# Compressed attention on column and row groups of TensorE, and a last piece without splitting and attention steps

## The chip, the cores and the metric

The kernel runs on one core of a Trainium2 chip. The metric is device time in microseconds (us), the median of several executions of the same program. A core has a matrix engine (TensorE; PE in the profile, with the loading of weights as PEld), a vector engine (VectorE, DVE), a scalar engine (ScalarE, ACT), a general one (GpSimd, POOL) and a queue engine (SyncE, SP) that issues the DMAs here. TensorE writes to PSUM only, eight banks of 128 x 512 float32; VectorE and ScalarE read the banks out.

## The reference

Two layers of a decoder trunk on 256 tokens of width 2048, all in float32. Each layer normalises its input, projects it to 6992 columns, runs four groups of four heads (128 wide), multiplies each group by a gate, projects back and adds the normalised result to the input:

```python
h = rms_norm(x, pre_g)
p = split_columns(h @ w_in + b_in)
o_sb  = stick_breaking_attention(...)      # group A
o_nsa = native_sparse_attention(...)       # group B
o_fox = forgetting_attention(...)          # group C
o_mla = latent_attention(...)              # group D
mix = concatenate([o_g * silu(gate_g) for each group])
return x + rms_norm(mix @ w_out, post_g)
```

Group B is the one that the change touches. It adds three branches, each with a gate per token and head. The compressed branch first makes 15 short keys and values out of blocks of 32 tokens (two small matrix products per block), and then attends to them:

```python
zc = einsum("bqhd,bnd->bhqn", qb, kc) * scale            # n: 15 compressed keys
pc = masked_softmax(zc, cmp_end[None, :] <= qpos[:, None])
o_cmp = einsum("bhqn,bnd->bqhd", pc, vc)
...
return gb[..., 0:1] * o_cmp + gb[..., 1:2] * o_slc + gb[..., 2:3] * o_win
```

The selected branch (o_slc) and the window branch (o_win) are plain causal attention at this length.

## The kernel before, in words

**Weight matmuls.** The large products use weights that are split into two parts, `whi` and `wlo`, so that TensorE can take them in its faster float32 form. A piece is 256 rows by 512 columns of weights. SP loads it into one of four `raw` buffers, ScalarE rounds each half (128 rows) to `whi`, VectorE subtracts to `wlo`, and TensorE uses the piece: 2.8 us of matmuls. Eight split pieces fit on chip. The class `Stream` keeps the counts: `his` and `los` are the halves split so far, `used` the pieces taken by TensorE, `loaded` the pieces asked for. When both halves of a piece are split, its raw buffer is free and SP loads the next piece (`loads`); small loads that wait in `side`, the compression's first weights among them, go out one with each piece.

A chunk of 512 columns of the input projection is eight pieces. There are two kinds. A transposed chunk (`t_group`, blocks "T", lines L634 and L635) has four blocks of 128 columns; each block has a PSUM bank of its own, and in each piece it takes two pairs of matmuls, 512 and 256 columns streamed. In the last piece (`ks == 7`) the blocks are finished one after the other, and `evac` reads each bank out: ScalarE copies one half (`tpart`), VectorE adds the other (`tgrp`), POOL multiplies by the norm factor. Then a task is spawned that adds the bias on ScalarE, and this reads POOL's product. The other kind (`k_group`, blocks "K", line L646) has tokens on the partitions and two banks. There are four such banks (`mm`), used in turn. The chunk of the compressed tokens (`nsa_kv`) has two T blocks and one K2 block, and its evacuation has the bias in it.

The order of chunks in a layer: cq and ckv of the latent group (K, 8 pieces), nsa q (K), 4 pieces of small up projections, mlag (T), nsa window keys (K), compressed and selected tokens (T, T, K2), nsag (T), sb q (T), sb k (T), sb v (K), sbg (T), fox q (T), fox k (T), fox v (K), foxg (T); then the output projection, four columns of eight pieces (L646), whose pieces 7 and 8 want the products of the fox heads.

**Order of work.** The program is one list of instructions per engine, written out by a planner at build time. After each pair or triple of matmuls `pump` moves the planned TensorE time on, then calls `step`, which runs the next due step of one task (attention heads, biases, gates, softmax of the compressed branch), and `Stream.tick`, which may split one half of a piece. Due times come from a simple cost per instruction (`Timed`, `count`, `pe`); every instruction of VectorE, ScalarE and POOL is recorded at line L119 of the helper, so these are told apart by their tiles. Engines take their lists in order, so a step that waits holds up what stands behind it on its engine.

**The compressed branch** (`nsa_cmp`, `nsa_heads`). When the compressed keys `kcT` and the rotated queries `nqT` are there, eight matmuls (L1214, one per 128 tokens and head) load 128 columns of queries as weights and stream the 32 key columns, 32 columns of one bank each. VectorE adds the mask, takes the maximum, subtracts, ScalarE exponentiates, VectorE sums, inverts, multiplies by the gate and scales, POOL multiplies by the mask. In the next step two transposes (L1237) turn the result, and one copy brings it to `pcT`: partitions 32h to 32h+31 hold head h. Float32 matmuls are two instructions each, transposes one. Two lanes (`lanes`, one per pair of heads) then each take an `op` bank and an `sp` bank. For each head the lane does one matmul on 32 rows (L1253, `tile_position=(32 * h, 0)`), then attends in the selected and the window branch (`attend`: L748 scores, softmax, L780 transposes, L792 and L793 values), all into its `op` bank. Other small products that the text names: L1102, the compression's first product, 32 weight columns on four column groups; L748 on `rT`, the rotary part of the latent scores, 64 rows on two row groups.

Of the kernel before, what the change touches and what calls it, by code (L numbers as in the profile page):

```python
# [10 lines left out]
F32 = mybir.dt.float32  # L11
# [8 lines left out]
S = 256  # L20
P = 128
# [81 lines left out]
class Timed:  # L103


    def __init__(self, kr, eng, key, base, per):
        self.kr, self.eng, self.key, self.base, self.per = kr, eng, key, base, per
# [54 lines left out]
class Stream:  # L162
# [55 lines left out]
    def lo(self):  # L218
# [8 lines left out]
        if kk == 1:  # L227
            del self.raw[p]
            self.loads()

    def tick(self, n=1):
        top = 2 * min(self.freed + self.BUFS - self.spare, len(self.specs))
        for _ in range(n):
            late = self.los - 2 * self.used < 4
            if self.los < self.his - (self.his < top and not late) and (late or self.kr.behind("v") < LAG):
                self.lo()
            if self.his < top and (late or self.kr.behind("s") < LAG) and self.here():
                self.hi()
# [21 lines left out]
class Kernel:  # L260
# [4 lines left out]
    def __init__(self, nc, tc, a, pools):  # L265
        self.nc, self.tc, self.a = Engines(self, nc), tc, a
        self.__dict__.update(pools)
        self.pt = self.dep = 0.0
        self.clk = {"v": 0.0, "s": 0.0, "g": 0.0}
        self.tasks = []  # L270
        self.negr = None
        self.free = {"sp": 2, "op": 2}
        self.freed = []
        self.done = Done(self)
        self.cols_of, self.ncols_of, self.fb, self.ci = {}, {}, {}, {}
        self.hcat, self.turn = {}, {}


    def pump(self, ns):
        self.pt += ns  # L280
        self.step()
        self.ws.tick()

    def now(self, at=0.0):

# [273 lines left out]
    def chunk(self, blocks, evac):  # L559

        acc = self.accs(len(blocks))
        for ks in range(NK // 2):
            last = ks == NK // 2 - 1
            hi, lo = self.ws.get()
            for i, (b, o) in enumerate(zip(blocks, acc)):
                if b[0] == "T":
                    self.mm_t(o, hi, lo, b[1], ks)
                elif b[0] == "K":  # L570
                    self.mm_k(o[:, :b[3]], self.h_at(ks, b[1]), hi, lo, b[2], b[3], ks == 0, last)
                else:
                    for t in range(2):
                        self.mm_k(o[:, t * S:(t + 1) * S], self.h_at(ks, t), hi, lo, b[1], S, ks == 0 and t == 0, last)
                if last:
                    self.now()
                    evac(i, o)
            self.ws.free()

    def first_chunk(self, l, cols):  # L580
# [224 lines left out]
        self.split(self.mxh[g][:, hp * 2:hp * 2 + 2, :], self.mxl[g][:, hp * 2:hp * 2 + 2, :], m3)  # L805
        self.done.add((l, "mix", g, hp))

    def lanes(self, l, g, heads, need=(), banks=1):


        for hp in range(2):
            def lane(task, hp=hp):
                for key in need:
                    yield from self.until(task, key)
                yield from self.take(task, "op")
                yield from self.take(task, "sp", banks)
                o = self.bank("op")
                o = [o[:, hh * S:(hh + 1) * S] for hh in range(2)], o
                yield from heads(hp, o[0])
                self.give("sp", banks)  # L820
                yield from self.until(task, (l, "gate", g, hp))
                self.mix(l, g, hp, o[1])
                self.give("op")
            self.spawn(lane)
# [376 lines left out]
    def nsa_cmp(self, l):  # L1201

        nc = self.nc

        def probs(task):
            for key in ("cmp", "nsa_q"):
                yield from self.until(task, (l, key))
            yield from self.take(task, "sp")
            qT = self.nqT
            cp = self.bank("sp")  # L1210
            for t in range(2):
                for h in range(4):
                    a = (t * 4 + h) * 32
                    nc.tensor.matmul(cp[:, a:a + 32], qT[:, h * S + t * P:h * S + (t + 1) * P],  # L1214
                                     self.kcT[:, :32], start=True, stop=True)
            self.pe(1700)
            pc = self.t256("pc").rearrange("p (g n) -> p g n", n=32)
            for t in range(2):
                nc.vector.tensor_add(pc[:, t * 4:(t + 1) * 4, :],
                                     cp[:, t * 128:(t + 1) * 128].rearrange("p (h n) -> p h n", h=4),  # L1220
                                     self.c3("cadd", 2)[:, t, None, :].to_broadcast([P, 4, 32]))
            mx = self.sm.tile([P, 8], F32, name="cmx")
            nc.vector.tensor_reduce(mx, pc, axis=AX.X, op=OP.max)
            nc.vector.tensor_sub(pc, pc, mx[:, :, None].to_broadcast([P, 8, 32]))
            nc.scalar.activation(pc, pc, AF.Exp, scale=SCALE)
            su = self.sm.tile([P, 8], F32, name="csu")
            nc.vector.tensor_reduce(su, pc, axis=AX.X, op=OP.add)
            nc.vector.reciprocal(su, su)
            su2 = su.rearrange("p (t h) -> p t h", t=2)
            nc.vector.tensor_mul(su2, su2, self.br[:, :, :, 0])  # L1230
            nc.vector.tensor_mul(pc, pc, su[:, :, None].to_broadcast([P, 8, 32]))
            for t in range(2):
                nc.gpsimd.tensor_mul(pc[:, t * 4:(t + 1) * 4, :], pc[:, t * 4:(t + 1) * 4, :],
                                     self.c3("cmul", 2)[:, t, None, :].to_broadcast([P, 4, 32]))
            yield 0
            for t in range(2):
                nc.tensor.transpose(cp[:, t * P:(t + 1) * P],  # L1237
                                    pc[:, t * 4:(t + 1) * 4, :].rearrange("p h n -> p (h n)"), self.ident)
            self.pe(220)
            self.pcT = self.zp.tile([P, S], F32, name="pcT", bufs=1)  # L1240
            nc.vector.tensor_copy(self.pcT, cp[:, :S])
            self.give("sp")
            yield 0
            self.done.add((l, "nsa_c"))

        self.spawn(probs)

    def nsa_heads(self, nb):
        def heads(hp, o):
            for hh in range(2):  # L1250
                h = 2 * hp + hh
                r = slice(32 * h, 32 * h + 32)
                self.nc.tensor.matmul(o[hh], self.vc[r, :], self.pcT[r, :], start=(hh == 0), stop=False,  # L1253
                                      skip_group_check=True, tile_position=(32 * h, 0))
                self.pe(430)
                q = self.nqT[:, h * S:(h + 1) * S]
                yield from self.attend([([(q, self.nkT[:, 0, :])], o[hh], self.sel[:, 0, P:], self.sel[:, 1, P:],
                                         False, False, self.br[:, :, h, 1])], SCALE)
# [205 lines left out]
    def layer(self, l, xsrc, dst):  # L1464
# [7 lines left out]
        nb = self.k_group(l, CHUNKS[3])  # L1472
# [6 lines left out]
        self.nsa_kv(l)  # L1479
        self.nsa_keys(l, nb)  # L1480
        self.nsa_cmp(l)
        self.lanes(l, "nsa", self.nsa_heads(nb), [(l, "nsa_k"), (l, "nsa_c")])
        self.t_group(l, ci["nsag"], gate="nsa")
        q, qd = self.t_group(l, 124, scale=SCALE)
        k, kd = self.t_group(l, ci["sbqk"] + 4)
# [86 lines left out]
```

## Time and profile before

| | |
|---|---|
| median of 3 runs | 946.74 us (946.71 to 946.87) |
| the profiled execution's own time | 946.79 us |
| its span, first to last instruction | 944.7 us |
| mean granted TensorE clock over the span | 0.998 |
| PE busy | 922.3 us, 98% of the span, 5170 instructions |
| DVE, ACT, POOL busy | 63%, 55%, 14% |
| DMA | 178.7 MB, mean 189 GB/s |

Busy is the time in which at least one instruction of an engine is under way. Matmuls overlap in the pipeline, so the mean duration of one is longer than the distance from its start to the next start; the latter is what a stream of matmuls costs. In the lists of instructions a row gives start, duration, engine, line, operation, tiles written and read, shape and count; a bracket behind it gives the idle time of the engine just before and what ended it.

### The profile page before, as it was taken

How to read it: one execution, taken by the hardware profiler on the slowest of the kernel's cores; microseconds unless marked ns; L12 is line 12 of the kernel's file. 1: busy time of each engine (PE TensorE's matmuls, PEld its weight loads, DVE VectorE, ACT ScalarE, POOL GpSimd, SP SyncE). 2: the span in 40 equal slices, each digit the busy share in tenths (PEclk: the TensorE clock that was granted, in tenths of full speed). 3: DMA queues.
4: the chain of work that ended last, by engine and by line, in shares of the span. 5: the costliest groups of instructions: out<-in, count | busy, mean ns of one | idle time of the engine just before them, and what ended most of it. 6: DMA issues, size and time to landing. Idle time of an engine off the chain costs nothing.

```text
span 944.7 us, 14519 instructions
## 1 busy us (share of the span) xinstructions
PE 922.3 (98%) x5170; PEld 783.0 (83%) x5170; DVE 598.7 (63%) x1293; ACT 519.2 (55%) x1170; POOL 133.3 (14%) x204
## 2 busy tenths in 40 slices
PE   7999999999999999999999999999999999999996
PEld 6888988777888888888878998887778888888885
DVE  6776757646666655754586867676366675567552
ACT  7745644645467563754476564555255775457540
POOL 0231011012011212100002310212010221020000
PEclk9999999999999999999999999999999999999999
DMA  8857746784454755489268577287744545746852
GB/s 271 264 177 193 216 139 182 238 256 125 118 160 125 242 190 156 149 275 309 93 200 271 159 188 228 78 249 227 224 115 131 156 142 183 232 146 200 281 187 89
DMA packets 118080, 178.70 MB, mean 189 GB/s; under 512 B 15996, under 2 KB 40568, under 8 KB 118008
## 3 DMA queue, kind: packets, MB, share of 16 engines
q1 hardware_dynamic: 118008, 177.78, 60.5%
q8 instruction: 40, 0.66, 0.3%
q14 instruction: 32, 0.26, 0.1%
HBM read 173.55 MB, written 4.20 MB: 188 GB/s over the span
## 4 chain that ended last, share of the span: by engine, by line
PE 86%; DMA 5%; DVE 4%; ACT 2%; POOL 1%; issue 1%; SPq 1%; POOLq 0%; DVEq 0%; ACTq 0%
PE mm L646 41%; PE mm L634 22%; PE mm L635 11%; PE sp L748 2%; DMA w<-nsa_cmp_w_v 2%; PE mm L942 2%; DVE wlo L119 2%; PE op L792 1%; DMA raw<-w_in 1%; PE sp L780 1%; DMA fcum<-frow 1%; DMA w<-nsa_cmp_w_k 1%; PE op L793 1%; PE sp L482 1%; ACT whi L119 1%
## 5 line engine op out<-in xcount | busy, mean ns | idle before, releaser
L119 DVE TENSOR_TENSOR wlo<-raw,whi 128x512 fp32r<-128x512 f32 (+2 forms) x592 | 389.2, 702 | 66.7 <-ACT whi L119 64.4
L634 PE MATMUL mm<-hcat,whi 128*128 128x512 f32 x1088 | 397.3, 406 | 1.7 <-DVE tgrp L119 1.3
L119 ACT ACTIVATE whi<-raw 128x512 fp32r<-128x512 f32 (+2 forms) x592 | 330.1, 613 | 118.5 <-DMA raw<-w_in 66.7
L635 PE MATMUL mm<-hcat,wlo 128*128 128x256 f32 x1088 | 304.3, 280 | 0.0
L634 PEld LDWEIGHTS mm<-hcat,whi 128*128 128x128 f32 x1088 | 204.6, 188 | 51.1 <-issue 3.7
L646 PE MATMUL mm<-whi,hcat 128*128 128x512 f32 (+2 forms) x768 | 230.5, 371 | 0.8 <-DVE tgrp L119 0.8
L635 PEld LDWEIGHTS mm<-hcat,wlo 128*128 128x128 f32 x1088 | 205.4, 189 | 0.4
L646 PEld LDWEIGHTS mm<-whi,hcat 128*128 128x128 f32 x768 | 139.2, 189 | 22.4 <-DVE tgrp L119 2.0
L646 PE MATMUL mm<-wlo,hcat 128*128 128x512 f32 (+2 forms) x384 | 139.1, 362 | 1.4 <-DVE wlo L119 1.3
L646 PE MATMUL mm<-whi,mxh 128*128 128x512 f32 x256 | 99.8, 390 | 0.0
L646 PE MATMUL mm<-whi,mxl 128*128 128x512 f32 x256 | 99.6, 389 | 0.0
L646 PE MATMUL mm<-wlo,mxh 128*128 128x512 f32 x256 | 99.6, 389 | 0.0
L646 PEld LDWEIGHTS mm<-wlo,hcat 128*128 128x128 f32 x384 | 72.7, 189 | 11.8 <-DVE wlo L119 3.0
L119 POOL TENSOR_TENSOR tgrp<-tgrp,rr 128x256 f32<-128x256 f32 x64 | 59.6, 955 | 162.2 <-DVE tgrp L119 162.0
L119 ACT ACTIVATE z<-z,nm 128x128 f32<-128x128 f32 x64 | 28.5, 447 | 55.2 <-DVE nm L119 54.1
L646 PEld LDWEIGHTS mm<-whi,mxl 128*128 128x128 f32 x256 | 48.0, 188 | 10.1
L646 PEld LDWEIGHTS mm<-whi,mxh 128*128 128x128 f32 x256 | 48.1, 188 | 10.0
L646 PEld LDWEIGHTS mm<-wlo,mxh 128*128 128x128 f32 x256 | 48.1, 188 | 9.8
L119 DVE TENSOR_TENSOR tgrp<-mm,tpart 128x256 f32<-128x256 f32 x64 | 26.0, 419 | 40.3 <-ACT tpart L119 40.0
L119 ACT ACTIVATE tpart<-mm 128x256 f32<-128x256 f32 x68 | 24.6, 381 | 40.7 <-PE mm L635 38.7
L119 DVE TENSOR_TENSOR y<-mm,bct 128x512 f32<-128x512 f32 x16 | 11.1, 692 | 48.1 <-ACT junk L119 48.1
L119 ACT ACTIVATE junk<-mm 128x512 f32<-128x512 f32 x16 | 9.6, 598 | 52.4 <-PE mm L646 52.4
(212 smaller groups left out, 766.7 us busy)
## 6 DMA issues: line engine op xcount, KB each, us to landing
raw<-w_in SPq DMA_DIRECT2D x207, 512.0 KB
raw<-w_out SPq DMA_DIRECT2D x64, 512.0 KB
x<-x SPq DMA_DIRECT2D x24, 256.0 KB
raw<-w_in SPq DMA_DIRECT2D x16, 268.0 KB
w<-nsa_cmp_w_k SPq DMA_DIRECT2D x8, 512.0 KB
w<-nsa_cmp_w_v SPq DMA_DIRECT2D x8, 512.0 KB
raw<-mla_w_uq SPq DMA_DIRECT2D x6, 384.0 KB
bct<-b_in SPq DMA_DIRECT2D x8, 256.0 KB
```

The lines of the kernel that those rows point to most:

```text
L119: return f(out, *args, **kw)
L482: nc.tensor.transpose(ps[:, k * P:(k + 1) * P], x[:, k * P:(k + 1) * P], self.ident)
L634: nc.tensor.matmul(o, wh, h, start=(ks + kk == 0), stop=False, skip_group_check=True)
L635: nc.tensor.matmul(o[:, :S], wl, h[:, :S], start=False, stop=last, skip_group_check=True)
L646: nc.tensor.matmul(o, x, w, start=(first and kk == 0 and i == 0), stop=(last and kk == 1 and i == 2), skip_group_check=True)
L748: nc.tensor.matmul(sp[:, a:a + s1], q[:, q0:q0 + P], k[:, :s1], start=(i == 0 and a == 0), stop=(i == n - 1), skip_group_check=True)
L780: nc.tensor.transpose(sp[:, i * P:(i + 1) * P], z[:, i * P:(i + 1) * P], self.ident)
L792: nc.tensor.matmul(o, v0, pt[:, :256], start=start, stop=False, skip_group_check=True)
L793: nc.tensor.matmul(o[:, 128:256], v1, pt[:, 256:384], start=False, stop=stop, skip_group_check=True)
L942: nc.tensor.matmul(o, a, b, start=(i == 0 and o is first[0]), stop=(i == len(mms) - 1), skip_group_check=True)
```

## The change

In `nsa_cmp` the scores are turned around: four matmuls, one per head, load the 32 key columns as weights and stream the head's 256 query columns. Each writes 32 partitions of the same bank columns, on its own column group of the array. VectorE copies the result out, two more transposes bring tokens to the partitions, and the softmax goes on as before with the heads in the order 0, 2, 1, 3; the gate is multiplied in two instructions. After the softmax `pcT` is 64 partitions by 512 columns, written by two copies: partitions 32hp to 32hp+31 and column half hh hold head 2hp+hh. A new task `nsa_open` takes both `op` banks and opens each with one matmul on 32 rows and 512 columns (row groups 0 and 32); the lanes get their bank from it and do no value matmul of their own. In `chunk`, `hold` is true while a T block of the last piece is computed; then `pump` runs neither a step nor a tick, unless `short` says that fewer than three pieces beyond the one in use are split.

```diff
--- before.py
+++ after.py
@@ -228,6 +228,10 @@
             del self.raw[p]
             self.loads()
 
+    def short(self):
+
+        return self.los - 2 * self.used < 6
+
     def tick(self, n=1):
         top = 2 * min(self.freed + self.BUFS - self.spare, len(self.specs))
         for _ in range(n):
@@ -269,6 +273,7 @@
         self.clk = {"v": 0.0, "s": 0.0, "g": 0.0}
         self.tasks = []
         self.negr = None
+        self.hold = False
         self.free = {"sp": 2, "op": 2}
         self.freed = []
         self.done = Done(self)
@@ -278,8 +283,9 @@
 
     def pump(self, ns):
         self.pt += ns
-        self.step()
-        self.ws.tick()
+        if not self.hold or self.ws.short():
+            self.step()
+            self.ws.tick()
 
     def now(self, at=0.0):
 
@@ -565,6 +571,8 @@
             last = ks == NK // 2 - 1
             hi, lo = self.ws.get()
             for i, (b, o) in enumerate(zip(blocks, acc)):
+
+                self.hold = last and b[0] == "T"
                 if b[0] == "T":
                     self.mm_t(o, hi, lo, b[1], ks)
                 elif b[0] == "K":
@@ -575,6 +583,7 @@
                 if last:
                     self.now()
                     evac(i, o)
+            self.hold = False
             self.ws.free()
 
     def first_chunk(self, l, cols):
@@ -805,16 +814,17 @@
         self.split(self.mxh[g][:, hp * 2:hp * 2 + 2, :], self.mxl[g][:, hp * 2:hp * 2 + 2, :], m3)
         self.done.add((l, "mix", g, hp))
 
-    def lanes(self, l, g, heads, need=(), banks=1):
+    def lanes(self, l, g, heads, need=(), banks=1, opened=None):
 
 
         for hp in range(2):
             def lane(task, hp=hp):
                 for key in need:
                     yield from self.until(task, key)
-                yield from self.take(task, "op")
+                if opened is None:
+                    yield from self.take(task, "op")
                 yield from self.take(task, "sp", banks)
-                o = self.bank("op")
+                o = self.bank("op") if opened is None else opened[hp]
                 o = [o[:, hh * S:(hh + 1) * S] for hh in range(2)], o
                 yield from heads(hp, o[0])
                 self.give("sp", banks)
@@ -1208,16 +1218,22 @@
             yield from self.take(task, "sp")
             qT = self.nqT
             cp = self.bank("sp")
+
+            for h in range(4):
+                g = 64 * (h % 2) + 32 * (h // 2)
+                nc.tensor.matmul(cp[g:g + 32, :S], self.kcT[:, :32], qT[:, h * S:(h + 1) * S], start=True, stop=True,
+                                 tile_position=(0, g), skip_group_check=True)
+            self.pe(650)
+            cs = self.t256("cs")
+            nc.vector.tensor_copy(cs, cp[:, :S])
+            yield 0
             for t in range(2):
-                for h in range(4):
-                    a = (t * 4 + h) * 32
-                    nc.tensor.matmul(cp[:, a:a + 32], qT[:, h * S + t * P:h * S + (t + 1) * P],
-                                     self.kcT[:, :32], start=True, stop=True)
-            self.pe(1700)
+                nc.tensor.transpose(cp[:, S + t * P:S + (t + 1) * P], cs[:, t * P:(t + 1) * P], self.ident)
+            self.pe(220)
             pc = self.t256("pc").rearrange("p (g n) -> p g n", n=32)
             for t in range(2):
                 nc.vector.tensor_add(pc[:, t * 4:(t + 1) * 4, :],
-                                     cp[:, t * 128:(t + 1) * 128].rearrange("p (h n) -> p h n", h=4),
+                                     cp[:, S + t * 128:S + (t + 1) * 128].rearrange("p (h n) -> p h n", h=4),
                                      self.c3("cadd", 2)[:, t, None, :].to_broadcast([P, 4, 32]))
             mx = self.sm.tile([P, 8], F32, name="cmx")
             nc.vector.tensor_reduce(mx, pc, axis=AX.X, op=OP.max)
@@ -1227,7 +1243,9 @@
             nc.vector.tensor_reduce(su, pc, axis=AX.X, op=OP.add)
             nc.vector.reciprocal(su, su)
             su2 = su.rearrange("p (t h) -> p t h", t=2)
-            nc.vector.tensor_mul(su2, su2, self.br[:, :, :, 0])
+            for hh in range(2):
+                nc.vector.tensor_mul(su2[:, :, 2 * hh:2 * hh + 2], su2[:, :, 2 * hh:2 * hh + 2],
+                                     self.br[:, :, hh:hh + 3:2, 0])
             nc.vector.tensor_mul(pc, pc, su[:, :, None].to_broadcast([P, 8, 32]))
             for t in range(2):
                 nc.gpsimd.tensor_mul(pc[:, t * 4:(t + 1) * 4, :], pc[:, t * 4:(t + 1) * 4, :],
@@ -1237,22 +1255,37 @@
                 nc.tensor.transpose(cp[:, t * P:(t + 1) * P],
                                     pc[:, t * 4:(t + 1) * 4, :].rearrange("p h n -> p (h n)"), self.ident)
             self.pe(220)
-            self.pcT = self.zp.tile([P, S], F32, name="pcT", bufs=1)
-            nc.vector.tensor_copy(self.pcT, cp[:, :S])
+            self.pcT = self.t512("pcT")[:64, :]
+            for hh in range(2):
+                nc.vector.tensor_copy(self.pcT[:, hh * S:(hh + 1) * S], cp[64 * hh:64 * hh + 64, :S])
             self.give("sp")
             yield 0
             self.done.add((l, "nsa_c"))
 
         self.spawn(probs)
+
+    def nsa_open(self, l, nb, need):
+
+
+        def opening(task):
+            for key in need:
+                yield from self.until(task, key)
+            yield from self.take(task, "op", 2)
+            os = [self.bank("op") for _ in range(2)]
+            for hp in range(2):
+                r = slice(32 * hp, 32 * hp + 32)
+                self.nc.tensor.matmul(os[hp], self.vc[r, :], self.pcT[r, :], start=True, stop=False,
+                                      skip_group_check=True, tile_position=(32 * hp, 0))
+            self.pe(1200)
+            self.lanes(l, "nsa", self.nsa_heads(nb), opened=os)
+            yield 0
+
+        self.spawn(opening)
 
     def nsa_heads(self, nb):
         def heads(hp, o):
             for hh in range(2):
                 h = 2 * hp + hh
-                r = slice(32 * h, 32 * h + 32)
-                self.nc.tensor.matmul(o[hh], self.vc[r, :], self.pcT[r, :], start=(hh == 0), stop=False,
-                                      skip_group_check=True, tile_position=(32 * h, 0))
-                self.pe(430)
                 q = self.nqT[:, h * S:(h + 1) * S]
                 yield from self.attend([([(q, self.nkT[:, 0, :])], o[hh], self.sel[:, 0, P:], self.sel[:, 1, P:],
                                          False, False, self.br[:, :, h, 1])], SCALE)
@@ -1479,7 +1512,7 @@
         self.nsa_kv(l)
         self.nsa_keys(l, nb)
         self.nsa_cmp(l)
-        self.lanes(l, "nsa", self.nsa_heads(nb), [(l, "nsa_k"), (l, "nsa_c")])
+        self.nsa_open(l, nb, [(l, "nsa_k"), (l, "nsa_c")])
         self.t_group(l, ci["nsag"], gate="nsa")
         q, qd = self.t_group(l, 124, scale=SCALE)
         k, kd = self.t_group(l, ci["sbqk"] + 4)
```

## Rows read from the trace of the kernel before

**Rows 1.** The page, busy time, share of the span and instructions of each engine.
```profile
PE 922.3 (98%) x5170; PEld 783.0 (83%) x5170; DVE 598.7 (63%) x1293; ACT 519.2 (55%) x1170; POOL 133.3 (14%) x204
```

**Rows 2.** Waits of TensorE by releaser: total us, times, longest us.
```profile
PE op L1102 <- DMA w<-nsa_cmp_w_v: 2.3, 4, 0.8
...
PE mm L646 <- DVE wlo L119: 1.3, 1, 1.3
PE mm L634 <- DVE tgrp L119: 1.3, 2, 0.6
PE sp L1237 <- POOL pc L119: 0.9, 2, 0.5
PE mm L646 <- DVE tgrp L119: 0.8, 1, 0.8
```

**Rows 3.** Timeline of TensorE, the score matmuls in layer 0.
```profile
211.34 0.28 PE L635 MATMUL mm<-hcat,wlo 128*128 128x256 f32 x1
211.46 1.87 PE L1214 MATMUL sp<-cmp,nqT 128*128 128x32 f32 x16
...
213.48 0.27 PE L635 MATMUL mm<-hcat,wlo 128*128 128x256 f32 x1
```

**Rows 4.** Timeline of TensorE, value matmul with scores behind it; values alone; scores alone.
```profile
220.88 0.27 PE L635 MATMUL mm<-hcat,wlo 128*128 128x256 f32 x1
221.09 0.69 PE L1253 MATMUL op<-pcT,cmp 32*128 32x256 f32 x2
...
222.28 0.58 PE L646 MATMUL mm<-whi,hcat 128*128 128x512 f32 x1
...
230.51 0.59 PE L792 MATMUL op<-pt,sn 128*128 128x256 f32 x2
230.94 0.27 PE L793 MATMUL op<-pt,sn 128*128 128x128 f32 x1
...
231.62 0.40 PE L646 MATMUL mm<-whi,hcat 128*128 128x512 f32 x1
231.85 0.82 PE L748 MATMUL sp<-sn,nqT 128*128 128x128 f32 x4
232.32 0.58 PE L646 MATMUL mm<-whi,hcat 128*128 128x512 f32 x1
```

**Rows 5.** Timeline of TensorE, two row groups (L748 on rT) and four column groups (L1102).
```profile
119.37 0.93 PE L748 MATMUL sp<-rT 64*128 64x128 f32 x8
120.22 0.38 PE L646 MATMUL mm<-whi,hcat 128*128 128x256 f32 x1
...
206.26 0.28 PE L635 MATMUL mm<-hcat,wlo 128*128 128x256 f32 x1
206.38 0.40 PE L634 MATMUL mm<-hcat,whi 128*128 128x512 f32 x1
206.61 0.28 PE L635 MATMUL mm<-hcat,wlo 128*128 128x256 f32 x1
206.82 0.64 PE L1102 MATMUL op<-w,blk 128*32 128x128 f32 x16
...
207.73 0.28 PE L635 MATMUL mm<-hcat,wlo 128*128 128x256 f32 x1
```

**Rows 6.** Timeline of TensorE, the pair of transposes in layer 1.
```profile
686.14 0.38 PE L1237 MATMUL sp<-ident,pc 128*128 128x128 f32 x2
```

**Rows 7.** Timeline of TensorE, sb q to sb k in layer 1.
```profile
653.63 0.27 PE L635 MATMUL mm<-hcat,wlo 128*128 128x256 f32 x1
654.53 0.50 PE L634 MATMUL mm<-hcat,whi 128*128 128x512 f32 x1 [0.63 <-DVE tgrp L119]
```

**Rows 8.** Timeline of ScalarE, the same stretch.
```profile
653.24 0.51 ACT L119 ACTIVATE tgrp<-tgrp,cols 128x256 f32<-128x256 f32 x1 [1.69 <-POOL tgrp L119]
```

**Rows 9.** Instructions on tile wlo by stretch: length, busy (x count), PEclk, DMA share, GB/s.
```profile
0.00:159.40 159.40, 93.91 (x304) 57.81 (x304) 66.19 (x106) 1.00 0.69 210
...
0.00:380.30 380.30, 225.90 (x752) 142.28 (x753) 157.34 (x239) 1.00 0.62 190
```

## The prediction

> **What bounds the kernel now.** I read the page's busy times first: TensorE is busy 98% of the span, VectorE 63%, ScalarE 55% [rows 1], and the granted clock is at its full level of 2.4 GHz (1.00 in the stretches of [rows 9]). So the first question for any edit is how much TensorE time it takes out; work on another engine counts only where TensorE waits for it. The list of TensorE's waits, read second, says where that is: a few places of one to three microseconds in total, each with its releaser [rows 2]. Third I read TensorE's timeline around the lines that the change touches. To price an insertion I take the time from the start of the last weight matmul before it to the start of a weight matmul behind it, less the undisturbed steps: 0.12 us from a 256-column weight matmul to the next start and 0.23 us from a 512-column one (206.26, 206.38, 206.61 in [rows 5]).
>
> **Part 1, the compressed branch on column and row groups.** Old price per layer. The eight score matmuls (L1214; 16 instructions, each loads 128 columns of weights to stream 32): 211.34 to 213.48 is 2.14 us, less 0.12 + 0.23, so 1.78 us [rows 3]. The four value matmuls (L1253) each stand ahead of four L748 instructions: 220.88 to 222.28 less 0.12 is 1.28 us. The same four L748 alone cost 231.62 to 232.32 less 0.23, 0.47 us, so one value matmul costs 0.81 us. Of that, two passes of 256 columns are 0.43 us (L792 shows two, 230.51 to 230.94), and 0.38 us is getting into the 32-row form and out of it [rows 4]. Together 1.78 + 4 x 0.81 = 5.02 us per layer.
>
> New price per layer. (a) Four score matmuls, 32 weight columns each, 256 streamed columns, on four column groups. The trace has this form with 128 streamed columns: L1102, 16 instructions, 206.61 to 207.73 less 0.35, 0.77 us [rows 5]. A pass of 128 columns is half of 0.215, so 16 of them in line would be 1.7 us: the four groups run side by side, four rounds of 0.11 or 0.43 us, with 0.34 us of entry and exit. The new form is two rounds of 0.215, again 0.43 + 0.34 = 0.77 us. With no overlap at all it is 8 x 0.215 + 0.34 = 2.06 us. (b) Two more transposes: the pair at L1237 is done in 0.38 us from the first start to the last end, one of them still in the pipe when the next matmul starts [rows 6]. I take two passes of 0.11, 0.22 us; bounds 0.1 and 0.4. (c) Two value matmuls of 512 columns on two row groups, each into its own bank. The nearest row is L748 on rT: 64 rows, two row groups, two banks, eight instructions, of which four stream 128 and four 256 columns. In line they would be 1.30 us; the next matmul starts after 0.85 us [rows 5], which is half of 1.30 and 0.2 more. So row groups overlap too. Two rounds of 512 columns are 0.86 us; with the 0.38 us of entry and exit 1.24 us; in line 2.10 us. New sum 0.77 + 0.22 + 1.24 = 2.23 us, or 4.38 us with no overlap. The gain is 2.79 us per layer, 5.6 us in all; the floor is 1.3 us.
>
> What this part adds elsewhere lies beside TensorE: two copies and one small multiply on VectorE, at its mean of 598.7 / 1293 = 0.46 us some 1.4 us per layer, on an engine that is idle 37% of the time [rows 1]. It costs something only where a transpose reaches TensorE before the copy or product that it reads. The trace has that once, at L1237, where POOL's product came late: 0.9 us of waiting in the two transposes of layer 0 [rows 2], nothing in layer 1 (the pair of [rows 6] has no wait before it). The branch has one step more now, and its steps are put off in a last piece; that can spare this wait or add one in the other layer. I take 0, bounds -0.9 and +1.3. The opening takes both `op` banks at once where each lane took one; what is queued behind it are the two lanes alone, which need both open anyway.
>
> The Trainium skill, page TensorE: Matmul & The Clock Gate, section Part 3: Packing small matmuls — row/col tiling, says that a weight load overlaps running matmuls only where its row group differs. All column groups use the same rows, so by that rule the eight passes of (a) stand in line with their weight loads (an estimate from the page: 32 columns over 1.2, 27 ns each), 8 x 0.242 + 0.34 = 2.3 us. The 16 passes of L1102 in 0.77 us [rows 5] speak against it; it is kept as a rival.
>
> **Part 2, nothing but evacuation in the last piece.** At the end of a transposed chunk ScalarE and VectorE empty four banks, one every 0.7 us (two pairs of 0.35), and the next transposed chunk wants the first of them at once, 2.1 us after its matmuls, and then one every 0.7 us. Now a task step slips in between. At 653.24 ScalarE runs the bias of block 0, for which it waited 1.69 us until POOL's product was there, and the evacuation of block 1 stands behind it in ScalarE's queue [rows 8]. TensorE then finds its bank unread: 653.63 to 654.53 is 0.90 us where 0.12 is due, so 0.78 us, of which 0.63 are shown as waiting [rows 7] and 0.15 are the restart. The list has two such waits of L634 for tgrp, 1.3 us, and one of L646, 0.8 us [rows 2]; with three restarts 1.3 + 0.8 + 0.5 = 2.6 us. With no step in that stretch ScalarE has nothing else to wait for, and 2.1 us is room for two short instructions. I take all 2.6 us; bounds 0 and 3.2 (the wait for cmpT, whose bias is part of the evacuation itself and stays, may shrink too).
>
> What covers the splitting that is put off is the lead of split pieces. At 380.30, when the last piece of the last input chunk begins, 239 halves are split and 116 pieces begun, so 3.5 pieces are ready; at 159.40 it is 106 halves and 52 pieces, one piece [rows 9]. `short` lets the splitting go on where fewer than three are ready, so the hold does not act at the second place, and at the first the lead falls by at most one piece of 2.8 us to 2.5. That hides it; with a lead under one, each half would show as a wait of 1.3 us, like the one for `wlo` in [rows 2]. The steps of the forgetting heads that are put off in that piece end in the output projection, whose seventh and eighth piece want them, 16 and 19 us in (12 matmuls of 0.23 us a piece): room for 2.8 us.
>
> What is late next are the loads of the compression's first weights. TensorE waits for the values' part four times, 2.3 us [rows 2], and part of that stands behind two of the removed waits. If these loads do not come sooner, the 0.8 us before them is only waited for later, in both layers 1.6 us. If the raw buffers behind which they are queued come free with the faster evacuation, nothing is lost. I take half, +0.8 us; bounds +3 (a held half gives its raw buffer back a piece later, and the loads behind it on SP's queue start later) and -1.
>
> **Sum.** -5.6 - 2.6 + 0 + 0.8 = -7.4 us. The profiled execution took 946.79 us (span 944.7), the median of the runs is 946.74, so both give the same base: 939.4 us.
>
> **Rivals.**
> 1. The groups do not overlap in the new shapes (longer streams; 32 rows instead of 64). Part 1 then gives 1.3 us and the time is 946.8 - 1.3 - 1.8 = 943.7 us. Against it stand L1102 and rT. By the page's rule, in (a) alone, 1.5 us a layer are lost: 939.4 + 3.0 = 942.4 us. Chance of the two together 0.08.
> 2. The waits for banks come back as others, the loads (+2.2 over what I took) and POOL (+1.3): 942.9 us. Or the hold does not do what it says, because `short` is true at most chunk ends, and part 1 alone is left: 941.2 us. For it, the four waits for w1; against it, the lead at 380.30. Chance 0.17.
> 3. Slower: splits that were put off come too late, and TensorE waits for `wlo` behind chunk ends, 1.3 us each. Eighteen chunks have transposed blocks. It takes six such waits to eat the 7.4 us and eight to be slower by more than a measurement can tell; at ten the time is 952 us. For it, the lead of one piece at 159.40; against it, 3.5 pieces, 9.8 us of matmuls, at 380.30. Chance 0.05.
>
> **How the numbers follow.** Forecast 0.70, by itself 936 to 942 (the bounds of the hold and the loads). For 8 in 10 I reach over rivals 1 and 2: 935.5 to 943.5. What a measurement here can tell from no change is 0.2%, 1.9 us, so faster is all below 944.9: the forecast and nearly all of rivals 1 and 2, 0.93; same 0.03; slower 0.04.
>
> **What would show it.** The scores' group costs 0.8 us instead of 1.78, and the values are one group of 1.2 us per layer instead of four of 0.8. The waits of L634 and L646 for tgrp are gone from the list, and in a last piece no bias stands between two evacuations. The prediction is wrong if TensorE waits for `wlo` behind chunk ends, if the waits of L1102 for its loads pass 6 us, or if the new groups take the 2 us that they would in line.

## The result and the profile after

The changed kernel takes 935.35 us (934.27 to 937.24, 4 runs), against 946.74 us before: a ratio of 0.988 (95% interval 0.9866 to 0.989), 11.4 us less. Forecast were 939.4 us and a range of 935.5 to 943.5. The direction was right and the two mechanisms were those named; the gain was 4 us larger than the forecast, and the time lies just below the range.

The page of the profile after, busy times (its span is 935.5 us):

```profile
PE 916.1 (98%) x5150; PEld 780.7 (83%) x5150; DVE 592.6 (63%) x1299; ACT 521.9 (56%) x1170; POOL 118.7 (13%) x204
```

TensorE is as much the bound as before [rows 1]; there is only less of it. The lines have moved: L634 is now L643, L646 is L655, L1102 is L1112, L1237 is L1255; the scores (L1214 before) are L1224, the new transposes L1231, the values (L1253 before) L1277.

TensorE's timeline in layer 0, the new groups: start, duration, engine, line, operation and tiles.

```profile
211.44 0.27 PE L644 MATMUL mm<-hcat,wlo 128*128 128x256 f32 x1
211.65 0.64 PE L1224 MATMUL sp<-nqT,cmp 128*32 128x256 f32 x8
212.21 0.50 PE L643 MATMUL mm<-hcat,whi 128*128 128x512 f32 x1
212.55 0.28 PE L644 MATMUL mm<-hcat,wlo 128*128 128x256 f32 x1
...
212.90 0.28 PE L644 MATMUL mm<-hcat,wlo 128*128 128x256 f32 x1
213.02 0.38 PE L1231 MATMUL sp<-ident,cs 128*128 128x128 f32 x2
213.16 0.48 PE L643 MATMUL mm<-hcat,whi 128*128 128x512 f32 x1
213.47 0.28 PE L644 MATMUL mm<-hcat,wlo 128*128 128x256 f32 x1
...
221.12 0.39 PE L655 MATMUL mm<-whi,hcat 128*128 128x512 f32 x1
221.44 1.13 PE L1277 MATMUL op<-pcT,cmp 32*128 32x512 f32 x4
222.49 0.50 PE L655 MATMUL mm<-whi,hcat 128*128 128x512 f32 x1
222.83 0.40 PE L655 MATMUL mm<-wlo,hcat 128*128 128x512 f32 x1
```

Priced as in [rows 3 to 5], the scores cost 211.44 to 212.55 less 0.35, 0.76 us. The pair of transposes delays the next matmul from 213.02 to 213.16 and that one's successor by 0.08 more (213.47, where 213.39 would be undisturbed), 0.22 us. The values cost 221.12 to 222.49 less 0.23 and, with 0.11 behind them (222.83 instead of 222.72), 1.25 us. Forecast were 0.77, 0.22 and 1.24. The Trainium skill (TensorE: Matmul & The Clock Gate, Part 3: Packing small matmuls — row/col tiling) says that weight loads overlap running matmuls only where the row groups differ. By the prediction's estimate from that rule the scores would have cost 2.3 us. The trace does not bear the rule out for column groups, and the measurement decides: the eight weight loads of the scores start between 211.64 and 211.69, while the first four matmuls, started at 211.65 to 211.67, run until 212.05 (single records of the trace, which the view merges into one row).

TensorE's waits after, by releaser: total us, times, longest.

```profile
PE op L1112 <- DMA w<-nsa_cmp_w_v: 3.0, 4, 1.5
...
PE mm L655 <- DVE wlo L119: 1.5, 2, 1.3
...
PE mm L655 <- DVE tgrp L119: 0.3, 1, 0.3
PE op L1112 <- DMA w<-nsa_cmp_w_k: 0.2, 1, 0.2
```

Beside [rows 2], the waits of 2.1 us for tgrp are down to 0.3, the 0.9 us for POOL at the transposes of pc is gone, the 0.3 us each for cmpT and z are gone, and the loads of w take 3.2 us, where the list before had 3.7 (2.3 for the values' part and 1.4 for the keys'). ScalarE in the last piece of sb q, layer 0, after:

```profile
187.70 0.38 ACT L119 ACTIVATE tpart<-mm 128x256 f32<-128x256 f32 x1 [0.33 <-PE mm L644]
188.39 0.39 ACT L119 ACTIVATE tpart<-mm 128x256 f32<-128x256 f32 x1 [0.32 <-PE mm L644]
189.10 0.38 ACT L119 ACTIVATE tpart<-mm 128x256 f32<-128x256 f32 x1 [0.33 <-PE mm L644]
189.38 0.50 ACT L119 ACTIVATE tgrp<-tgrp,cols 128x256 f32<-128x256 f32 x1
```

Each evacuation now waits for its own matmuls and for nothing else. The bias, which stood between two of them in [rows 8], comes behind the fourth and finds POOL's product ready. [rows 8] is of layer 1; there the four evacuations now start at 646.99, 647.68, 648.38 and 649.07, and the first bias at 649.35.

The profiled execution itself took 937.24 us, the longest of the four. What most of that may have come from stands at the end.

### The profile page after: what moved, and what is told of

Same layout as the page of the kernel before. It is cut to its first block, busy times and chain, and to the rows that moved or that the text cites. A ratio compares the mean times of both kernels' runs of the same rounds, so it can differ in the third digit from the quotient of the medians.

```text
span 935.5 us, 14485 instructions
## 1 busy us (share of the span) xinstructions
PE 916.1 (98%) x5150; PEld 780.7 (83%) x5150; DVE 592.6 (63%) x1299; ACT 521.9 (56%) x1170; POOL 118.7 (13%) x204
## 4 chain that ended last, share of the span: by engine, by line
PE 89%; DMA 4%; DVE 4%; ACT 1%; issue 1%; SPq 0%; POOL 0%; DVEq 0%; POOLq 0%; ACTq 0%
PE mm L655 42%; PE mm L643 24%; PE mm L644 12%; PE sp L757 3%; DMA w<-nsa_cmp_w_v 2%; DVE wlo L119 2%; PE mm L952 2%; PE op L801 1%; DMA raw<-w_in 1%; PE sp L789 1%; PE op L802 1%; PE op L1112 1%; PE sp L488 1%; DMA w<-nsa_cmp_w_k 1%; DMA x<-x 0%
## 5 line engine op out<-in xcount | busy, mean ns | idle before, releaser
L119 DVE TENSOR_TENSOR wlo<-raw,whi 128x512 fp32r<-128x512 f32 (+2 forms) x592 | 377.0, 684 | 69.6 <-ACT whi L119 68.3
L643 PE MATMUL mm<-hcat,whi 128*128 128x512 f32 x1088 | 398.4, 406 | 0.1
L643 PEld LDWEIGHTS mm<-hcat,whi 128*128 128x128 f32 x1088 | 204.5, 188 | 49.7 <-issue 4.7
L655 PE MATMUL mm<-whi,hcat 128*128 128x512 f32 (+2 forms) x768 | 229.1, 371 | 0.3 <-DVE tgrp L119 0.3
L655 PEld LDWEIGHTS mm<-whi,hcat 128*128 128x128 f32 x768 | 140.0, 190 | 22.6 <-issue 2.2
L655 PE MATMUL mm<-wlo,hcat 128*128 128x512 f32 (+2 forms) x384 | 139.4, 363 | 1.5 <-DVE wlo L119 1.5
L655 PE MATMUL mm<-whi,mxh 128*128 128x512 f32 x256 | 100.4, 392 | 0.0
L655 PE MATMUL mm<-whi,mxl 128*128 128x512 f32 x256 | 99.7, 389 | 0.0
L655 PE MATMUL mm<-wlo,mxh 128*128 128x512 f32 x256 | 99.6, 389 | 0.0
L655 PEld LDWEIGHTS mm<-wlo,hcat 128*128 128x128 f32 x384 | 73.0, 190 | 11.9 <-DVE wlo L119 2.7
L119 POOL TENSOR_TENSOR tgrp<-tgrp,rr 128x256 f32<-128x256 f32 x64 | 51.5, 832 | 146.2 <-DVE tgrp L119 146.0
L655 PEld LDWEIGHTS mm<-whi,mxl 128*128 128x128 f32 x256 | 48.1, 188 | 10.1
L655 PEld LDWEIGHTS mm<-whi,mxh 128*128 128x128 f32 x256 | 48.1, 188 | 9.7
L655 PEld LDWEIGHTS mm<-wlo,mxh 128*128 128x128 f32 x256 | 48.1, 188 | 9.6
L119 ACT ACTIVATE pt<-sp 128x384 f32<-128x384 f32 x32 | 15.3, 490 | 36.7 <-PE sp L789 36.7
```

The source lines that it names most:

```text
L119: return f(out, *args, **kw)
L643: nc.tensor.matmul(o, wh, h, start=(ks + kk == 0), stop=False, skip_group_check=True)
L655: nc.tensor.matmul(o, x, w, start=(first and kk == 0 and i == 0), stop=(last and kk == 1 and i == 2), skip_group_check=True)
```

## The experiments

Every kernel was timed beside the kernel before; ratios are to it, with 95% intervals. There were three such groups of measurements: the next four kernels, then the four with only steps, only splits, column groups only and loads two ahead, then the other four. The kernel before itself had medians of 946.6, 948.5 and 946.3 us in them, so kernels of different groups are compared by their ratios. TensorE's idle time, below, is the span of a profile less its busy time of PE: 22.4 us before, 19.5 us in the next profile.

**The changed kernel once more.**

> The changed kernel once more, beside the others. The profile of it had 1.4 us in a stretch at a lower granted clock (480 to 490 us: 0.86) and 0.6 us more at the start; without them I expect 934.3 to 936. Theory: the gain of 11.4 us is 5.6 us of TensorE instructions in the compressed branch, some 3.1 us of bank waits (tgrp, cmpT), 1.3 us of the wait for POOL at the pc transposes, 1.0 us of waits for z in the last piece of foxg, and 0.4 us of the weight loads. Rival: the groups gave more than 5.6 us and the hold less than 5.

Measured 935.18 us, ratio 0.9881 (0.9868 to 0.9895). Its profile has a span of 934.4 us (PE busy 914.9), no stretch at a lower clock ahead of the tail, and 3.9 us of waits for w. So the gain of 11.3 to 11.4 us holds.

**The groups alone.**

```diff
-                self.hold = last and b[0] == "T"
+                self.hold = False
```

> The new compressed branch, no hold. Theory: 5.6 us from the instructions, and the waits for tgrp and z stay: 941.2 us; 939.9 if the wait for POOL goes because the branch has one step more. Rival (the groups gave more than their instructions): under 939.

Measured 942.34 us, ratio 0.9959 (0.9946 to 0.9971), 4.3 us less than before. The instructions cost what they cost in the changed kernel, but the waits for banks grew:

```profile
PE mm L643 <- DVE tgrp L119: 2.8, 4, 0.8
...
PE mm L655 <- DVE tgrp L119: 1.6, 1, 1.6
...
PE sp L1255 <- POOL pc L119: 0.5, 1, 0.5
```

For tgrp that is 4.4 us instead of the 2.1 of [rows 2]. But the waits for w fell from 3.7 to 1.6 us at the same time, and the idle time in all is 22.4 us as before. So 5.6 us of instructions were worth 4.3 by themselves (3.9 by the ratio), the time was 1.1 us above the theory's, and the rival (under 939) is out; what took the rest is not shown by the waits.

**The hold alone.**

```diff
...
     def pump(self, ns):
         self.pt += ns
-        self.step()
-        self.ws.tick()
+        if not self.hold or self.ws.short():
+            self.step()
+            self.ws.tick()
...
```

> The compressed branch as before, with the hold. Theory: bank waits 3.1, z 1.0, so 942.6 us; 941.3 if the wait for POOL goes because the transposes are put off behind the last piece. Rival (the hold gives only the three tgrp waits of the list): 944.1 us. If the two parts add, this and the groups alone together come to 11.4 us.

Measured 940.1 us, ratio 0.9937 (0.9923 to 0.9951): 6.5 us less (6.0 by the ratio), more than either theory gave. TensorE's list has no wait for tgrp, cmpT or z left, 0.5 us for POOL and 2.4 us for w, which is 1.3 us less than before:

```profile
PE op L1111 <- DMA w<-nsa_cmp_w_v: 1.3, 3, 0.6
PE op L1111 <- DMA w<-nsa_cmp_w_k: 1.1, 1, 1.1
PE sp L1246 <- POOL pc L119: 0.5, 1, 0.5
```

The two parts alone come to 4.3 + 6.5 = 10.8 us, both together to 11.4 (by the ratios 9.8 and 11.3): within the intervals they add, and the hold is the larger of the two.

**The bias behind the chunk**, in the kernel before.

```diff
...
             if gate is None:
-                self.spawn(bias)
+                held.append(bias)
...
         self.chunk([("T", h * P) for h in range(4)], evac)
+        for f in held:
+            self.spawn(f)
```

> The kernel before, with one edit: the bias tasks of a transposed chunk are spawned behind the chunk and not in its last piece; splitting and all other steps stay. Theory (a bias that waits for POOL in ScalarE's list holds up the next evacuation): the two waits of L634 for tgrp go, 1.8 us, the one of L646 (softmax of the compressed branch) stays: 945.0 us. Rival (VectorE's splits between the evacuations are what makes them late): the waits stay, 946.7 us.

Measured 943.22 us, ratio 0.9971 (0.9959 to 0.9982). As the theory had it, the two waits of L634 are gone and the one of L646 is still there at 0.8 us. Splitting goes on between evacuations: in the last piece of sb q, layer 0, VectorE runs a split (`wlo`) at 187.61 between the adds of the first block (187.27) and of the second (188.21), and TensorE does not wait there:

```profile
PE mm L646 <- DVE tgrp L119: 0.8, 1, 0.8
PE sp L1240 <- POOL pc L119: 0.5, 1, 0.5
...
PE mm L634 <- DVE cmpT L119: 0.3, 1, 0.3
```

The gain is 3.4 us (2.7 by the ratio) where 1.8 was expected; the wait for z and part of the one for POOL went too. So one task in the wrong place in ScalarE's list is about half of what the hold gives.

**Only the steps held**, splitting goes on.

```diff
         if not self.hold or self.ws.short():
             self.step()
-            self.ws.tick()
+        self.ws.tick()
```

> The changed kernel, but in the last piece only the task steps are held; the splitting goes on there. Theory (a step that waits in ScalarE's or VectorE's list, a bias or a softmax, is what holds up the evacuation, and a step of the fox heads is what makes TensorE wait for z): as the changed kernel, 935 to 936.5 us, no waits of L643 for tgrp. Rival (splits of 0.6 and 0.7 us between the evacuations matter as much): 2 us and more above it, with waits for tgrp.

Measured 938.68 us, ratio 0.9902 (0.9882 to 0.9922), some 2 us above the changed kernel, with intervals that overlap. There is no wait for tgrp in its list, though VectorE runs splits between the evacuations (`wlo` at 188.02 in layer 0, between adds at 187.68 and 188.62), so splits there do not make them late, and that part of the theory stands. The time expected (935 to 936.5) was missed, and where the 2 us lie is not shown: POOL's product is waited for again, 1.3 us, but the waits for w are 3.2 us in all against 3.9, and the idle time is 19.9 us against 19.5. In the profiled execution, the longest of the four (939.47), a wait of 2.0 us for w is followed by ten microseconds at a granted clock of 0.85 (200 to 210 us); the other three, at 0.998 over the whole span, still took 937.5 to 939.1.

**Only the splits held**, steps go on.

```diff
-        if not self.hold or self.ws.short():
-            self.step()
+        self.step()
+        if not self.hold or self.ws.short():
             self.ws.tick()
```

> The other half: only the splitting is held, the task steps go on. Theory: near the groups alone (942.3 us), 941 to 942.5, with waits of L643 for tgrp of 2 us and more in all. Rival: 938 us or less.

Measured 954.5 us, ratio 1.0066 (1.0042 to 1.0091): slower than before, and by the ratios 10 us behind the groups alone, which neither theory nor rival had. ScalarE at the end of sb q, layer 0:

```profile
190.13 0.51 ACT L119 ACTIVATE tgrp<-tgrp,cols 128x256 f32<-128x256 f32 x1 [1.31 <-POOL tgrp L119]
190.54 0.37 ACT L119 ACTIVATE tpart<-mm 128x256 f32<-128x256 f32 x1
192.22 0.51 ACT L119 ACTIVATE tgrp<-tgrp,cols 128x256 f32<-128x256 f32 x1 [1.31 <-POOL tgrp L119]
192.63 0.36 ACT L119 ACTIVATE tpart<-mm 128x256 f32<-128x256 f32 x1
194.30 0.51 ACT L119 ACTIVATE tgrp<-tgrp,cols 128x256 f32<-128x256 f32 x1 [1.30 <-POOL tgrp L119]
```

A bias stands behind every block, each waits 1.3 us for POOL, and the next evacuation stands behind it. TensorE then waits three times in a row, 0.2, 1.1 and 1.1 us. In [rows 8] only block 0's bias had slipped in. The planner's `step` lets no such task out while it sees VectorE or ScalarE more than 1 us behind, and with the splits gone it does not see that. By this reading the splits in the last piece had been keeping steps out of it; the rows show the order, the reason is read from the code and was not tested. Nor is it most of the loss. The idle time is 32.1 us, 9.7 more than with the groups alone; waits for tgrp make 0.7 of that (5.1 us against 4.4), waits for w 5.2 (6.8 against 1.6) and the copy of the scores 2.2 (against none). Why those grew no run shows.

**Column groups only**, values as four matmuls of 256 columns in the lanes.

```diff
...
-        self.nsa_open(l, nb, [(l, "nsa_k"), (l, "nsa_c")])
+        self.lanes(l, "nsa", self.nsa_heads(nb), [(l, "nsa_k"), (l, "nsa_c")])
```

> The changed kernel with the value matmuls as before: four per layer of 32 rows and 256 columns, in the lanes, 0.81 us each, instead of one group of 1.25 us. By the rows, 2 x (3.24 - 1.25) = 4.0 us more than the changed kernel: 939.3 us. Rival (the value matmuls on row groups gave nothing, their cost was hidden): 935 to 936.

Measured 941.21 us, ratio 0.9933 (0.991 to 0.9956): 5 us above the changed kernel by the ratios, 4.0 expected. The rival (935 to 936) is out.

**Row groups only**, scores as eight matmuls.

```diff
...
-            for h in range(4):
-                g = 64 * (h % 2) + 32 * (h // 2)
-                nc.tensor.matmul(cp[g:g + 32, :S], self.kcT[:, :32], qT[:, h * S:(h + 1) * S], ...)
...
+            for t in range(2):
+                for h in range(4):
+                    c = S + t * P + 64 * (h % 2) + 32 * (h // 2)
+                    nc.tensor.matmul(cp[:, c:c + 32], qT[:, h * S + t * P:h * S + (t + 1) * P],
+                                     self.kcT[:, :32], start=True, stop=True)
```

> The changed kernel with the scores as before (eight matmuls, 128 weight columns, 32 streamed), the heads put in the new order, and no second transposes. By the rows 2 x (1.78 - 0.76 - 0.22) = 1.6 us more than the changed kernel: 936.8 us. Rival (the shorter chain, one copy and one step less, pays for the longer matmuls): 935 us or less.

Measured 937.19 us, ratio 0.9897 (0.988 to 0.9914): 1.5 us above the changed kernel, 1.6 expected, though the intervals overlap.

**Both value matmuls on one row group.**

```diff
...
-                r = slice(32 * hp, 32 * hp + 32)
-                self.nc.tensor.matmul(os[hp], self.vc[r, :], self.pcT[r, :], ..., tile_position=(32 * hp, 0))
+                self.nc.tensor.matmul(os[hp], self.vc[:32, :], self.pcT[hp], ..., tile_position=(0, 0))
```

> The changed kernel, but both value matmuls of 512 columns use row group 0 (the probabilities of all heads are copied to partitions 0 to 31, by four copies instead of two). Theory (row groups run side by side): the four instructions stand in line, the group costs 2.1 us instead of 1.25 and the time is 1.7 us above the changed kernel, 936.9 us. Rival (one after the other anyway, the gain is that of fewer instructions): the group costs 1.25 us and the time stays at 935.2.

TensorE's timeline around them:

```profile
221.13 0.39 PE L655 MATMUL mm<-whi,hcat 128*128 128x512 f32 x1
221.45 1.98 PE L1278 MATMUL op<-pcT,cmp 32*128 32x512 f32 x4
223.35 0.50 PE L655 MATMUL mm<-whi,hcat 128*128 128x512 f32 x1
```

The group costs 221.13 to 223.35 less 0.23, and 0.1 behind it, 2.1 us in both layers, 0.85 more than on two row groups: row groups run side by side, and the rival falls. The time was 935.84 us, ratio 0.9889 (0.9872 to 0.9906), 0.8 us above the changed kernel and not 1.7, and within its interval. In this profile TensorE is busy 916.6 us, the expected 1.7 above the 914.9 of the changed kernel's second profile, but it waits 1.2 us for w, not 3.2 to 3.9, which would cover the rest.

**The loads of w two ahead**, and **later due times.**

```diff
...
-                    if q + 2 < 4:
-                        w1_load(q + 2)
+                    w1_load(i * 4 + q + 2)
```

> The changed kernel with one addition: the loads of the compression's first weights run two ahead across the border from keys to values too, where before the first two of the values were asked for when the keys were done. TensorE waits 3 us for them in the profiles of the changed kernel. If the request is late, most of that goes: 932.5 to 934 us. If the DMA queue is what is late (raw pieces ahead of them), the waits move and the time stays at 935 us.

Measured 935.92 us, ratio 0.9874 (0.9855 to 0.9894): as the changed kernel, where 932.5 to 934 was expected if the request had been late. The waits for w went from 3.9 to 3.1 us, and 1.1 us for POOL came back.

```diff
-                self.done.t[key] = self.nc.sync.came
+                self.done.t[key] = self.nc.sync.came + (2500 if key[1] == "w1" else 0)
...
-            yield 0
+            yield 2000
```

> The changed kernel with two due times moved and nothing else: a load of the compression's first weights is taken as landed 2.5 us later than the planner thought, and the transposes of pc come 2 us later. Theory: the 3.9 us that TensorE waits for these loads are a matter of order (the product stands in TensorE's list before its weights land, while weight matmuls that could run stand behind it); most of it goes, and no wait for POOL: 931.5 to 933.5 us beside 935.2 of the changed kernel. Rival (the DMA queue is the limit, so the pieces behind come late as well): 935 us, with waits for w or wlo.

Measured 934.9 us, ratio 0.9881 (0.9864 to 0.9898): no gain that can be told, where the theory had 931.5 to 933.5. The waits for w are gone altogether, and no others for w or wlo came for them, so they were a matter of order and not of the DMA rate; but 2.0 us of waits for tgrp and 1.4 us for POOL stand in their place.

> The same two due times on top of the loads that run two ahead. If order is what counts, as the one before, 931.5 to 933.5; if the earlier request also helps, 1 us less.

With both edits 933.46 us (933.25 to 933.6), ratio 0.9863 (0.9847 to 0.9879). TensorE's list inside the layers is nearly empty:

```profile
PE sp L1256 <- POOL pc L119: 0.5, 1, 0.5
...
PE mm L655 <- DVE tgrp L119: 0.3, 1, 0.3
PE mm L643 <- DVE kgrp L119: 0.2, 1, 0.2
```

Its idle time is 16.3 us. This is the fastest kernel of the study: every one of its runs is below the fastest of the changed kernel (933.93), but the two were not timed beside each other and their intervals overlap. So it is likely, and not shown, that the change left some 1.7 us on the table.

## Why the prediction was wrong in size, step by step

- **Part 1, 5.6 us: right.** The three groups cost 0.76, 0.22 and 1.25 us against 0.77, 0.22 and 1.24; the gain is 2.79 us per layer. (The old scores are 1.79 us by their rows and not 1.78, which changes nothing.) Reading a new form's price off its nearest relatives (L1102 for column groups, L748 on rT for row groups) held, and the one-row-group kernel shows that the overlap is real. What no row of before could show is that the groups alone are worth only 4.3 us. Their bank waits grew, their waits for w fell by about as much, and the reason for the missing 1.3 us stays open.
- **Part 2, 2.6 us: right in mechanism, too small.** The waits for tgrp fell as forecast (2.1 to 0.3 us). But the hold alone gives 6.5 us, of which 1.3 are waits for w that do not fall in the changed kernel. I had priced only the three waits for tgrp. The one for z (0.3 us, which I had seen in the last piece of foxg and left out) and the one for cmpT (0.3 us, taken only as a bound) went too, and each carries its restart of some 0.15 us: 0.9 us that no term had.
- **POOL's wait, 0 taken: this term failed.** I thought that it could be spared in one layer or added in the other. In the changed kernel it is gone in layer 0 and none came in layer 1, 0.9 us and two restarts: the transposes of layer 0 start at 219.05, in the chunk behind sb k, and POOL's product was done at 218.18. It depends on the order of everything else: 0.5 us remains with either part alone, and 1.1 to 1.5 us stand in four re-ordered kernels.
- **The loads of w, +0.8 taken: failed.** Their waits are 3.2 and 3.9 us in two profiles of the changed kernel, 3.7 before; nothing was given back. The kernel with later due times shows that they are an order that waits, not a queue that is full.
- **The sum.** 7.4 forecast, plus about 1.2 for POOL, 0.6 for the loads (0.2 more than before in the second profile, where 0.8 was taken), 0.9 for z and cmpT with their restarts, less 0.3 for the wait for tgrp that stays, gives 9.8 us. The difference of two spans without a clock dip ahead of the tail is 944.7 - 934.4 = 10.3 us, so 0.5 us stays open. The medians differ by 1.1 us more, nearly all of it because the profiled execution took 936.16 us, 1.0 above the median of its kernel; what makes executions differ is not shown. I had set the two uncertain terms at nothing and above it, and both fell below. Even with every bound at its good end the terms come to 5.6 + 3.2 + 0.9 + 1.0 = 10.7 us, 936.0 us, which the measured time is below: the bounds of the hold and of POOL left out z and the restarts. The range reached lower, to 935.5, and was missed by 0.15 us.
- **The rivals.** No overlap: refuted by the groups' prices. Waits that come back as others: not in the changed kernel, but bank or POOL waits did come back in five of its relatives (the groups alone, the two half holds, the loads two ahead and the later due times). That the hold does nothing (941.2 us): refuted by the hold alone. Late splits: no wait for `wlo` appeared behind a chunk end; the slower side did show up, by another way, where the splits are held and the steps are not.

## What to carry to other kernels

When an engine takes its list in order, look at what stands between two instructions that empty banks: a short instruction there that waits for a third engine cost the matrix engine more here than a long one that waits for nothing. An insertion into a dense stream of matmuls could be priced here to 0.02 us from the nearest form in the trace; the waits around it, which depend on the order of everything else, could not, and their bounds should be open on both sides by the whole of the waits in the list. Two halves of a rule that keeps work out of a stretch may only be good together: test each alone.

## What the runs showed of the hardware

Float32 matmuls on several column or row groups interleave their two passes. In the single records of the changed kernel's trace, the first passes of the four column groups start within 0.02 us (211.645 to 211.665) and the second passes 0.24 us later (211.885 to 211.905). So eight instructions of 256 columns, in line 1.7 us, are through with entry and exit in 0.76 us. On two row groups the passes of 512 columns start at 221.44 in both and at 221.97 to 221.98 in both; on one row group the four start at 221.45, 221.98, 222.41 and 222.84, one behind the other.

The other thing was not expected: the granted clock fell in some executions after TensorE had waited, and not in others with the same wait. The changed kernel's profile waits 1.34 us for `wlo` at 478.70, and then (stretch: length, busy of PE, PEld, DVE, ACT and POOL, granted clock, DMA share, GB/s):

```profile
470.00:480.00 10.00, 8.47 (x42) 6.45 (x41) 9.75 (x24) 5.01 (x16) 0.49 (x1) 0.97 0.54 157
480.00:490.00 10.00, 10.00 (x44) 8.17 (x43) 6.33 (x18) 7.08 (x22) 0.02 (x1) 0.86 0.71 226
```

Its second profile, with a wait of 1.3 us at the same place:

```profile
470.00:480.00 10.00, 8.65 (x43) 6.60 (x42) 9.92 (x24) 5.37 (x17) 0.14 (x1) 1.00 0.51 158
480.00:490.00 10.00, 10.00 (x50) 8.27 (x49) 7.89 (x20) 8.54 (x25) 0.60 (x1) 1.00 0.83 260
```

From the matmul that waited to the same later one it is 4.19 us in the first (478.70 to 482.89) and 2.63 in the second (478.18 to 480.81), 1.6 us more, which would be most of what set that execution apart (937.24 against a median of 935.35). The kernel with only the splits held waits 3.2 us for w, until 672.11, and the 8 us behind that are granted 0.62:

```profile
672.00:680.00 8.00, 7.89 (x54) 6.08 (x55) 2.85 (x5) 3.23 (x6) 0.00 (x0) 0.62 1.11 346
```

A granted clock of 0.86 or 0.62 over such a stretch is a mixture of the clock's two levels, 2.4 and 1.2 GHz. So in the first of these executions a wait of 1.34 us was followed by a further loss of 1.6 us, and in the second a wait of the same length by none; what decides between them no run here shows.
